# Scaling keys and queries on VectorE alone in a hybrid decoder layer

## The chip, the cores and the metric

The kernel runs on one core of a Trainium2 chip. The core has a matrix engine (TensorE, PE in the profile), three engines for elementwise work (VectorE or DVE, ScalarE or ACT, GpSimd or POOL), a queue processor that issues transfers (SyncE or SP), and 16 DMA engines. The metric is device time in microseconds, lower is better.

## The reference

One decoder layer over 512 tokens of width 1024, in float32. A normalised input is projected to many columns at once; four token mixers of width 512 work on them (A: forgetting attention with 8 heads of 64, B: a gated linear recurrence, C: sparse attention with 8 query heads over 2 key heads, D: spatial gating), each is gated, projected back, merged by sigmoid gates, and a last projection is added to the input. What the change touches is the RMS normalisation of the attentions' queries and keys, each head's 64 values by themselves:

```python
def rms_norm(x, g):
    x32 = x.astype(jnp.float32)
    y = x32 * lax.rsqrt(jnp.mean(x32 * x32, axis=-1, keepdims=True) + NORM_EPS)
    return (y * g.astype(jnp.float32)).astype(x.dtype)
...
    y_a = fox_attention(rms_norm(heads(qa, FOX_HEADS), qn_a), rms_norm(heads(ka, FOX_HEADS), kn_a),
                        heads(va, FOX_HEADS), fa + b_forget).reshape(B, S, W)
    y_c = nsa_attention(rms_norm(heads(qc, NSA_HEADS), qn_c), ...
```

In attention C the keys of the selected and of the windowed branch are normalised the same way.

## The kernel before, in words

**Precision.** Every operand of a product is split into a high part, rounded for TensorE, and a low part, the difference; a product is high x high, high x low and low x high. For a weight the high part (`hi_cast`) is a copy by GpSimd or ScalarE and the low part a VectorE subtraction in two halves of 512 columns (`wsplit`, tiles `w_...` from `r_...`). Both inputs of that subtraction lie in SBUF.

**Stages.** The projections to `ka`, `qa` and `va` come first, from about 6 to 78 us, 128 tokens to a PSUM bank. `emit_z` copies each bank to `zk_a` or `zq_a`, squares it and sums the squares of each head. `fox_scales` turns the sums into reciprocal square roots (tile `tsa`, a run of short VectorE instructions) and multiplies each token block of `zk_a` (lines 729 to 732: 128 partitions, 8 heads of 64) and of `zq_a` by its scales, in place. In the same region `gate_block` computes the forget gate's logarithms (`fa`) and their running sum, the scan that writes `negc`, a part of the tile `y_a`; its value goes into rows of the keys' operand `kb_a`.

Attention A then runs head by head (`fox_units`, `attend`) from about 77 to 180 us. Its TensorE instructions are interleaved with those of dense projections that don't depend on it: `kv`, `qc`, `cm`, `vd`. For a head: keys and queries are transposed on TensorE (`kt_a`, `qt_a`), scores go to `s_a`, VectorE adds the mask and takes the minimum of the negated scores (`p_a`, `nm_a`), ScalarE takes the exponential, GpSimd scales the rows, TensorE transposes them (`tb`), ScalarE and VectorE split them (`ph_a`, `pl_a`), TensorE multiplies with the values into the one bank of `o_a`. `evict` empties that bank: ScalarE copies one half (`ol_a`), VectorE adds the other (`y_a`); only then may the next head write to the bank.

Attention C's keys (`zk_c`, a part of the tile `zkm`, 4 heads) and queries (`zq_c`, 8 heads) come out of the `kv` and `qc` projections in that time. Once the last `qc` block is there, the generator `nsa_scales` is put on the list `side`, whose generators advance between matmuls; it computes the scales (tile `tsc`) and multiplies, token block by token block, `zk_c` (256 columns) and `zq_c` (512 columns). TensorE transposes them (`kt_s`, `kt_w`, `qt_c`) once attention A is done.

**What sets the order.** From line 609 to line 1390 an instruction isn't issued where it is written: `Order.add` notes it with what it depends on, and `Order.settle` issues a region after `Order.plan` has ordered each engine's queue. The plan takes four drafts of a list schedule; each draft takes on every engine the instruction that is due first, by a due time worked back from TensorE's order in the draft before. Costs are in `Order.cost`. An instruction of GpSimd other than a memset, or of VectorE with an SBUF input and none in PSUM, is taken to hold a shared port, so that the draft lets one engine begin after the other's instruction. The lines of it that bear on the scalings:

```python
        if name == "DVE":
            alone = bool(wide) and method not in ("tensor_reduce", "reciprocal", "memset") and not any(
                x.tensor.name in self.psum for x in wide)
            return 0.155 + free / 960 + 0.05 * scalar + 0.06 * (method == "tensor_tensor_scan" and free / 100), alone
...
        return (0.09 + free / 540 if len(wide) > 1 and method == "tensor_tensor" else 0.18 + free / 1170), True
```

On TensorE a draft takes, of the instructions that are ready, the one that the program text has first. On the chip the engines run their queues in order and wait for each other by semaphores. From about 365 us on the order is that of the program text.

**Transfers.** SP issues the weights' loads, each behind the VectorE subtraction that frees its buffer. GpSimd issues the transfers that add in memory (`dmg0s`, `dmg2s` and the like), paced by TensorE's progress.

In the profile nearly all instructions of the ordered region carry line 290, that of the issuing call, so tiles tell them apart. The functions that the change touches:

Of the kernel before, what the change touches and what calls it, by code (L numbers as in the profile page):

```python
# [14 lines left out]
ALU = mybir.AluOpType  # L15
# [3 lines left out]
P = 128  # L19
# [306 lines left out]
def tile_hybrid_layer(ctx: ExitStack, tc: tile.TileContext, x, xT, units, small, bsp, out):  # L326
    nc = tc.nc
    order = Order(nc)
    ACT, DVE, POOL, PE, DMA = (_Engine(order, e) for e in ("ACT", "DVE", "POOL", "PE", "SP"))
# [259 lines left out]
    def rsqrt(v, y, t):  # L589

        I32 = mybir.dt.int32
        DVE.tensor_scalar(t.bitcast(I32), v.bitcast(I32), 1, None, op0=ALU.logical_shift_right)
        DVE.tensor_scalar(y.bitcast(I32), t.bitcast(I32), -1.0, float(0x5F3759DF), op0=ALU.mult, op1=ALU.add)
        for _ in range(3):
            DVE.tensor_tensor(t, y, y, op=ALU.mult)
            DVE.scalar_tensor_tensor(t, t, -0.5, v, op0=ALU.mult, op1=ALU.mult)
            DVE.scalar_tensor_tensor(y, t, 1.5, y, op0=ALU.add, op1=ALU.mult)
# [104 lines left out]
    zk_a = rp.tile([P, 4, S], F32, name="zk_a")  # L702
    zq_a = rp.tile([P, 4, S], F32, name="zq_a")
# [19 lines left out]
    def fox_scales():  # L723
        DVE.tensor_tensor(ssa, ssa, rstd[:, 1, :].unsqueeze(2).to_broadcast([P, 4, 16]), op=ALU.mult)
        DVE.tensor_scalar(ssa, ssa, EPS, None, op0=ALU.add)
        y = tsa[:, 0, :].rearrange("p (t h) -> p t h", t=4)
        rsqrt(ssa, y, tsa[:, 1, :].rearrange("p (t h) -> p t h", t=4))
        DVE.tensor_tensor(y, y, rstd[:, 0, :].unsqueeze(2).to_broadcast([P, 4, 16]), op=ALU.mult)
        for t in range(4):
            for z, c0, eng in ((zk_a, 0, POOL), (zq_a, 8, DVE)):  # L730
                zv = z[:, t, :].rearrange("p (h d) -> p h d", h=8)
                eng.tensor_tensor(zv, zv, y[:, t, c0:c0 + 8].unsqueeze(2).to_broadcast([P, 8, 64]), op=ALU.mult)

# [92 lines left out]

    run(gv, 8)
    fox_scales()
    gate_block()
    run(gv)  # L830
# [159 lines left out]
    def nsa_scales():  # L990
        DVE.tensor_scalar(ssc, ssc, 1.0 / 64, EPS, op0=ALU.mult, op1=ALU.add)
        y_ = tsc[:, 0, :].rearrange("p (t h) -> p t h", t=4)
        rsqrt(ssc, y_, tsc[:, 1, :].rearrange("p (t h) -> p t h", t=4))
        yield 0.0
        for t in range(4):
            for z, c0, n in ((zk_c, 0, 4), (zq_c, 4, 8)):
                zv = z[:, t, :].rearrange("p (h d) -> p h d", h=n)
                POOL.tensor_tensor(zv, zv, y_[:, t, c0:c0 + n].unsqueeze(2).to_broadcast([P, n, 64]), op=ALU.mult)
                yield 0.0
                yield 0.0  # L1000

# [25 lines left out]
    def last_qc(t, ps):  # L1027
        emit_qc(t, ps)
        if t == 3:
            side.append(nsa_scales())  # L1030
# [957 lines left out]
```

## Time and profile before

| | |
|---|---|
| median of 3 runs (lowest to highest) | 695.24 us (694.14 to 695.49) |
| the profiled execution: its time, its span | 695.5 us, 693.8 us |
| mean granted TensorE clock | 0.997 |
| busy: TensorE, VectorE, ScalarE, GpSimd | 683.2, 553.4, 406.5, 209.4 us |
| GpSimd's scalings of `zk_a` | 4, 5.8 us |
| GpSimd's scalings of `zq_c` and `zkm` | 4 and 4, 4.9 and 3.0 us |
| VectorE's scalings of `zq_a` | 4, 5.0 us |

Busy times overlap, since the engines work side by side. A busy TensorE is not one at its peak, because matmuls are pipelined and their ends are modelled. The difference between the execution's time and its span, 1.7 us, lies around the profiled instructions. In the rows below, a group has its engine, operation, the tiles written and read (out<-in), shapes and count, then busy time and mean duration, then the idle time in front of it and what ended that. A row of a timeline has start and length in us; idle time before it stands in brackets with what ended it.

### The profile page before, as it was taken

How to read it: one execution, taken by the hardware profiler on the slowest of the kernel's cores; microseconds unless marked ns; L12 is line 12 of the kernel's file. 1: busy time of each engine (PE TensorE's matmuls, PEld its weight loads, DVE VectorE, ACT ScalarE, POOL GpSimd, SP SyncE). 2: the span in 40 equal slices, each digit the busy share in tenths (PEclk: the TensorE clock that was granted, in tenths of full speed). 3: DMA queues.
4: the chain of work that ended last, by engine and by line, in shares of the span. 5: the costliest groups of instructions: out<-in, count | busy, mean ns of one | idle time of the engine just before them, and what ended most of it. 6: DMA issues, size and time to landing. Idle time of an engine off the chain costs nothing.

```text
span 693.8 us, 9785 instructions
## 1 busy us (share of the span) xinstructions
PE 683.2 (98%) x3277; PEld 564.5 (81%) x3277; DVE 553.4 (80%) x1100; ACT 406.5 (59%) x766; POOL 209.4 (30%) x279
## 2 busy tenths in 40 slices
PE   8999999998999999999999999999999999999997
PEld 6888788886888787888887878888888888888886
DVE  6789788696668648889998579977889788858995
ACT  4563558574272237777666894355666665655861
POOL 4114864546445324534351121200202401300000
PEclk9999999999999999999999999999999999999999
DMA  8637176798869999964202225459999999896422
GB/s 310 256 122 242 40 203 212 225 218 234 249 183 318 253 312 221 247 167 106 62 31 77 78 89 188 162 187 358 252 331 311 366 317 363 234 339 207 132 90 92
DMA packets 35298, 145.44 MB, mean 210 GB/s; under 512 B 4128, under 2 KB 7584, under 8 KB 32032
## 3 DMA queue, kind: packets, MB, share of 16 engines
q1 hardware_dynamic: 30208, 108.67, 43.8%
q0 software_dynamic: 4608, 35.65, 24.0%
q10 hardware_dynamic: 432, 0.49, 0.3%
q8 instruction: 26, 0.43, 0.2%
q14 instruction: 24, 0.20, 0.1%
HBM read 139.56 MB, written 58.20 MB: 285 GB/s over the span
## 4 chain that ended last, share of the span: by engine, by line
PE 91%; ACT 3%; DVE 3%; POOL 1%; DMA 1%; issue 1%; SPq 0%; DVEq 0%; POOLq 0%; ACTq 0%
PE pj L302 4%; PE tb L290 3%; PE z_ka L290 3%; PE z_qc L290 3%; PE z_xb L290 3%; PE z_ga L290 3%; PE z_va L290 3%; PE z_vd L290 3%; PE z_gd L290 3%; PE z_gb L302 3%; PE z_qa L290 3%; PE z_ud L290 3%; PE z_kv L290 3%; PE o_s L290 3%; PE outy L302 3%; PE mg0y L302 2%
## 5 line engine op out<-in xcount | busy, mean ns | idle before, releaser
L302 POOL TENSOR_SCALAR mark<-mark 128x1 f32<-128x1 f32 x16 | 16.8, 1050 | 102.8 <-ACT mark L302 102.7
L302 DVE TENSOR_TENSOR w_mg<-r_mg,w_mg 128x512 fp32r<-128x512 f32 x48 | 31.8, 687 | 11.1 <-ACT w_mg L302 11.0
L302 PE MATMUL pj<-w_wb,yh 128*128 128x512 f32 x128 | 40.4, 390 | 0.0
L302 ACT CAST w_mg<-r_mg 128x1024 fp32r<-128x1024 f32 x24 | 25.2, 1049 | 10.3 <-issue 4.9
L290 POOL TENSOR_SCALAR p_s<-p_s,nm_s 128x512 f32<-128x512 f32 (+3 forms) x32 | 21.3, 681 | 22.4 <-DVE nm_s L290 18.5
L302 PEld LDWEIGHTS pj<-w_wb,yh 128*128 128x128 f32 x128 | 24.0, 188 | 4.9
L290 POOL TENSOR_SCALAR p_w<-p_w,nm_w 128x128 f32<-128x128 f32 (+3 forms) x32 | 18.4, 588 | 29.9 <-DVE nm_w L290 29.9
L290 ACT ACTIVATE p_s<-p_s,nm_s 128x512 f32<-128x512 f32 (+3 forms) x32 | 18.0, 562 | 13.6 <-DVE nm_s L290 13.2
L302 PE MATMUL pj<-w_wb,yl 128*128 128x512 f32 x64 | 25.4, 396 | 0.5 <-DVE yl L302 0.5
L290 ACT ACTIVATE p_w<-p_w,nm_w 128x256 f32<-128x256 f32 (+3 forms) x32 | 17.9, 562 | 12.4 <-DVE nm_w L290 12.3
L290 PE MATMUL z_xb<-xh,w_xb 128*128 128x512 f32 x64 | 24.6, 410 | 0.0
L290 POOL TENSOR_SCALAR p_a<-p_a,nm_a 128x128 f32<-128x128 f32 (+3 forms) x32 | 19.0, 607 | 16.5 <-DVE nm_a L290 16.4
L290 ACT CAST ph_a<-tb 128x512 fp32r<-128x512 f32 (+1 forms) x24 | 12.4, 516 | 19.3 <-PE tb L290 19.1
L290 PE MATMUL z_ud<-xh,w_ud 128*128 128x512 f32 x64 | 23.4, 405 | 0.0
L290 PE MATMUL z_gd<-xh,w_gd 128*128 128x512 f32 x64 | 22.6, 397 | 0.3 <-DVE sgd L290 0.3
L290 PE MATMUL z_ga<-xh,w_ga 128*128 128x512 f32 x64 | 21.9, 397 | 0.0
L302 DVE TENSOR_TENSOR w_wb<-r_wb,w_wb 128x512 fp32r<-128x512 f32 x28 | 18.5, 687 | 4.0 <-POOL w_wb L302 3.5
L302 PE MATMUL z_gb<-xh,w_gb 128*128 128x512 f32 x64 | 20.9, 390 | 0.0
L290 ACT ACTIVATE p_a<-p_a,nm_a 128x512 f32<-128x512 f32 (+3 forms) x32 | 17.9, 560 | 5.1 <-DVE nm_a L290 5.1
L302 POOL TENSOR_SCALAR w_wb<-r_wb 128x1024 fp32r<-128x1024 f32 x8 | 10.0, 1250 | 28.9 <-PE pj L302 13.9
L290 DVE CUSTOM_DVE_ANT_0 p_a<-s_a,maskm 128x512 f32<-128x512 f32 (+3 forms) x32 | 14.9, 486 | 4.6 <-PE tb L290 2.8
L290 ACT CAST ph_s<-tb 128x512 fp32r<-128x512 f32 (+1 forms) x24 | 12.2, 512 | 9.0 <-PE tb L290 8.7
(744 smaller groups left out, 2413.1 us busy)
## 6 DMA issues: line engine op xcount, KB each, us to landing
r_mg<-in_units_dram SPq DMA_DIRECT2D x16, 512.0 KB, 6.9
r_wb<-in_units_dram SPq DMA_DIRECT2D x12, 512.0 KB, 3.7
dmg<-in_units_dram POOLq DMA_DIRECT2D x4, 1024.0 KB, 9.7
r_mg<-dmg SPq DMA_DIRECT2D x8, 512.0 KB, 10.1
dmg0s<-in_units_dram POOLq DMA_DIRECT2D x3, 1024.0 KB, 10.5
dmg2s<-in_units_dram POOLq DMA_DIRECT2D x3, 1024.0 KB, 13.6
dmg1s<-in_units_dram POOLq DMA_DIRECT2D x3, 1024.0 KB, 11.4
r_mg0s<-dmg0s SPq DMA_DIRECT2D x6, 512.0 KB, 4.6
```

The lines of the kernel that those rows point to most:

```text
L290: getattr(self.eng[name], method)(*args, **kw)
L302: return lambda *args, **kw: real(*args, **kw).ins
```

## The change

The engine of twelve multiplications changes: in `fox_scales` those of `zk_a` (4 of 128 x 512), in `nsa_scales` those of `zk_c` and `zq_c` (4 of 128 x 256 and 4 of 128 x 512). Operands, shapes and the order in the program text stay; the order in the queues is planned anew from the changed program.

```diff
@@ fox_scales
         for t in range(4):
-            for z, c0, eng in ((zk_a, 0, POOL), (zq_a, 8, DVE)):
+            for z, c0, eng in ((zk_a, 0, DVE), (zq_a, 8, DVE)):
                 zv = z[:, t, :].rearrange("p (h d) -> p h d", h=8)
                 eng.tensor_tensor(zv, zv, y[:, t, c0:c0 + 8].unsqueeze(2).to_broadcast([P, 8, 64]), op=ALU.mult)
@@ nsa_scales
             for z, c0, n in ((zk_c, 0, 4), (zq_c, 4, 8)):
                 zv = z[:, t, :].rearrange("p (h d) -> p h d", h=n)
-                POOL.tensor_tensor(zv, zv, y_[:, t, c0:c0 + n].unsqueeze(2).to_broadcast([P, n, 64]), op=ALU.mult)
+                DVE.tensor_tensor(zv, zv, y_[:, t, c0:c0 + n].unsqueeze(2).to_broadcast([P, n, 64]), op=ALU.mult)
```

## The prediction

> **What bounds the kernel now.** I read the page first, for the engine that sets the end.
>
> ```profile
> span 693.8 us, 9785 instructions
> PE 683.2 (98%) x3277; PEld 564.5 (81%) x3277; DVE 553.4 (80%) x1100; ACT 406.5 (59%) x766; POOL 209.4 (30%) x279
> PE 91%; ACT 3%; DVE 3%; POOL 1%; DMA 1%; issue 1%; SPq 0%; DVEq 0%; POOLq 0%; ACTq 0%
> ```
>
> TensorE is busy for 98% of the span and is 91% of the chain that ends last. So time can only come from moments in which TensorE stands still or runs slowly, and the second view is its list of waits, of which these are the longest:
>
> ```profile
> PE o_a L290 <- DVE y_a L290: 2.7, 1, 2.7
> PE warm L302 <- DVE warm L302: 1.5, 1, 1.5
> PE tb L290 <- POOL p_w L290: 0.5, 1, 0.5
> ```
>
> The longest is one single wait of 2.7 us, for VectorE. Everything else is small or belongs to the start. The third view, busy time by stretches, shows what lies around it (columns: stretch, length, busy time and count of PE, PEld, DVE, ACT, POOL, then granted clock, DMA share, GB/s).
>
> ```profile
> 157.00:163.00 6.00, 3.34 (x19) 2.57 (x17) 5.94 (x9) 3.65 (x12) 3.49 (x5) 1.00 0.91 314
> 163.00:165.00 2.00, 1.93 (x9) 1.69 (x10) 1.63 (x3) 0.94 (x2) 1.09 (x1) 0.79 1.02 176
> 165.00:167.50 2.50, 2.50 (x7) 1.92 (x7) 0.69 (x1) 0.19 (x1) 2.50 (x6) 0.50 0.72 131
> 167.50:170.00 2.50, 2.50 (x16) 2.20 (x15) 0.13 (x1) 1.70 (x3) 2.50 (x4) 0.98 0.16 33
> 170.00:196.50 26.50, 26.50 (x125) 22.03 (x125) 14.94 (x38) 8.82 (x16) 8.51 (x16) 1.00 0.85 238
> 196.50:300.00 103.50, 102.52 (x533) 84.06 (x531) 79.67 (x200) 53.85 (x133) 46.11 (x59) 1.00 0.93 256
> 300.00:365.00 65.00, 64.89 (x374) 55.28 (x374) 61.49 (x173) 44.80 (x116) 27.21 (x43) 1.00 0.32 78
> ```
>
> After the gap the granted clock is 0.79, 0.50 and 0.98 before it is 1.00 again: the gap has a tail. Then TensorE runs without a gap to 196.5, and nearly so to 365. The fourth view, the timeline of single engines, tells what made VectorE late. TensorE:
>
> ```profile
> 159.96 0.39 PE L290 MATMUL z_cm<-xl,w_cm 128*128 128x512 f32 x1
> 163.07 0.47 PE L290 MATMUL o_a<-ph_a,v_a 128*128 128x512 f32 x1 [2.73 <-DVE y_a L290]
> ```
>
> VectorE, ScalarE and GpSimd:
>
> ```profile
> 157.07 3.97 DVE L290 TENSOR_TENSOR w_vd.01_961<-r_vd.01_960,w_vd.01_961 128x512 fp32r<-128x512 f32 x1
> 160.97 0.41 DVE L290 CUSTOM_DVE_ANT_0 p_a<-s_a,maskm 128x256 f32<-128x256 f32 x1
> 161.53 0.68 DVE L290 TENSOR_TENSOR w_vd.01_961<-r_vd.01_960,w_vd.01_961 128x512 fp32r<-128x512 f32 x1
> 162.24 0.68 DVE L290 TENSOR_TENSOR y_a<-o_a,ol_a 64x512 f32<-64x512 f32 x1
> ...
> 158.09 0.59 ACT L290 COPY ol_a<-o_a 64x512 f32<-64x512 f32 x1 [0.17 <-PE o_a L290]
> ...
> 157.03 0.91 POOL L290 TENSOR_TENSOR zkm<-zkm,tsc 128x256 f32<-128x256 f32 x1
> 157.61 1.32 POOL L290 TENSOR_TENSOR zq_c<-zq_c,tsc 128x512 f32<-128x512 f32 x1
> 158.61 0.89 POOL L290 TENSOR_TENSOR zkm<-zkm,tsc 128x256 f32<-128x256 f32 x1
> 159.18 1.31 POOL L290 TENSOR_TENSOR zq_c<-zq_c,tsc 128x512 f32<-128x512 f32 x1
> ```
>
> Here is the whole mechanism. The same subtraction takes 0.68 us at 161.53 and 3.97 us at 157.07. During the long one GpSimd runs four of the scalings that the change moves, from 157.03 to 160.49, and VectorE's instruction ends at 161.04, 0.55 us behind the last of them. In the queue behind it stand two score reductions, the second subtraction and y_a, which empties the one PSUM bank that the next head's values need. ScalarE had handed over its part at 158.68 (158.09 + 0.59); y_a starts only at 162.24.
>
> **The change part by part: the second attention (line 998).** The change takes eight scalings from GpSimd and gives them to VectorE.
>
> What goes. Without GpSimd's scalings the subtraction at 157.07 takes 0.68 and ends at 157.75. The two reductions take 0.56 (160.97 to 161.53), the second subtraction 0.68: VectorE reaches y_a at about 159.0 (later than ScalarE's 158.68, so VectorE decides) and ends it at 159.7. TensorE is busy until 160.35 (159.96 + 0.39), so it doesn't wait, with 0.65 us to spare. That is the 2.73 us. The clock's tail: a stretch of t us at clock c loses t(1 - c), so 2.0 x 0.21 + 2.5 x 0.50 + 2.5 x 0.02 = 0.42 + 1.25 + 0.05 = 1.72 us. The tail is contiguous with the gap and every later stretch shown has 1.00, so I let it go with the gap. Gain: 2.73 + 1.72 = 4.45 us.
>
> What comes. Eight multiplications on VectorE, bounded by these rows:
>
> ```profile
> L290 DVE TENSOR_TENSOR w_ga<-r_ga,w_ga 128x512 fp32r<-128x512 f32 x8 | 5.4, 698 | 3.2 <-POOL w_ga L290 2.5 <-ACT w_ga L290 0.7
> L290 DVE TENSOR_TENSOR sc<-sc,cm 128x256 f32<-128x256 f32 x8 | 3.5, 432 | 0.2
> L290 PE MATMUL kt_s<-identf,zkm x4: 272/272/273, 196.6 to 197.0; 128*128 128x128 f32 x4
> L290 PE MATMUL qt_c<-identf,zq_c x16: 270/272/273, 198.5 to 324.7; 128*128 128x128 f32 x16
> ```
>
> Four of 512 columns at 0.70 and four of 256 at 0.43 are 4.5 us. Their first readers are transposes on TensorE at 196.6 and 198.5, 39 us after GpSimd begins with them at 157.03. In the 33.5 us from 163.0 to 196.5 VectorE is busy 1.63 + 0.69 + 0.13 + 14.94 = 17.4 us, so 16 us are free: cover of three times the need, and I take 0 for them. Without cover they would cost up to 4.5 us, or, if each meets a GpSimd instruction as zq_a does below (1.53 for 512 columns; 0.91, GpSimd's slowest, for 256), 4 x 1.53 + 4 x 0.91 = 9.8 us. Below zero the cost can't go: they free nothing that this sum doesn't count already. No DMA is issued by the moved step; GpSimd's queue merely gets past it sooner.
>
> A page of the Trainium skill, "SBUF — State Buffer", section "Who interferes with whom", says that a VectorE instruction with two SBUF inputs and a GpSimd instruction that reads SBUF lock each other out, and that whoever is first holds the ports for one whole instruction. The row agrees with the lockout, not with its length: VectorE lost 3.3 us (3.97 - 0.68), and no single GpSimd instruction there lasted over 1.32. By the page alone 1.32 us of the delay would go and 2.0 stay, of which 1.3 us would still reach TensorE: a gain of some 1.4 us instead of 2.73, and 694.1. The end times (160.49 and 161.04) speak for all four scalings as the cause.
>
> **The first attention (lines 730 to 732).** Four of GpSimd's scalings join VectorE's four.
>
> ```profile
> L290 POOL TENSOR_TENSOR zk_a<-zk_a,tsa x4: 1478/1485/1487, 64.0 to 68.4; 128x512 f32<-128x512 f32 x4
> L290 DVE TENSOR_TENSOR zq_a<-zq_a,tsa x4: 691/1526/1532, 63.9 to 67.4; 128x512 f32<-128x512 f32 x4
> 63.92 5.04 DVE L290 TENSOR_TENSOR zq_a<-zq_a,tsa 128x512 f32<-128x512 f32 x4
> 71.30 1.21 DVE L290 TENSOR_TENSOR_SCAN y_a<-fm,fa 8x512 f32<-8x512 f32 x1 [0.69 <-ACT fa L290]
> 78.82 0.60 ACT L290 CAST kb_a<-y_a 8x512 fp32r<-8x512 f32 x1
> L290 PE MATMUL kt_a<-identf,zk_a x16: 271/272/273, 77.9 to 137.2; 128*128 128x128 f32 x16
> ```
>
> Both engines slow each other to about 1.5 us a piece now, so VectorE needs 5.04 us for four. Eight alone at the uncontended 0.691 of the same row are 5.5 us: VectorE is 0.5 us later at most, and GpSimd is free 5.8 us (68.4 + 1.49 - 64.0) earlier. Behind VectorE stand the forget gate's logarithm and its scan at 71.30; the scan ends at 72.51 and its reader starts at 78.82, so 6 us cover half a microsecond. TensorE reads zk_a at 77.9, 8 us after it is done now. Cost 0; if all four met GpSimd work at 1.53, another 3.4 us, still covered; a gain is excluded, since TensorE waits for nothing there.
>
> **Sum.** 695.5 us is the profiled execution's own time (span 693.8 and 1.7 around it), 0.3 above the median of 695.24. 695.5 - 4.45 = 691.05; I say 691.0. All later work follows TensorE, so it moves forward with it.
>
> **The rivals.**
>
> *The gap goes, the clock's tail stays.* If the tail had another cause, 695.5 - 2.73 = 692.8. For it: the gap is only 2.73 us long. Against: the tail begins where the gap ends, and the stretches shown from 170 on have none. "TensorE: Matmul & The Clock Gate" of the Trainium skill, section "What's actually happening", lets the clock fall after an idle window of about 3.4 us, which by its letter this gap doesn't fill; it calls that window free-running. Chance 0.06.
>
> *Only part of the gain arrives, or it is given back.* The transfers could take it: their share is 0.85 to 0.93 from 170 to 300, and weights that land no earlier would make TensorE wait for what it no longer waits for at 160; then 695.5. Against: no TensorE wait above names a DMA. The plan of the whole region is also drawn anew, with VectorE busy 61.49 of 65 us from 300 to 365; one new gap of about 2.7 us with its tail would give the gain back too. Chance 0.15, centre 695; the 694.1 of the shorter lockout lies in it.
>
> *Slower: the scalings are queued ahead of y_a.* The scales are ready by 157.03, where VectorE has 0.65 us to spare. All eight there at 4.5 us give y_a's end at 164.2 and a gap of 3.9 against 2.73 now, with the tail 1.2 us slower: 696.7. Contended at 9.8 us the gap is 9.2 us: 6.4 us slower, 702. It decides from 0.65 + 2.73 = 3.4 us of scalings in front of y_a. For it: the plan already puts the w_vd.01 subtractions there, though other work could go first. Against: the plan ranks by due time, and 196.6 is late. Chance 0.11.
>
> *More is gained.* GpSimd, freed at 64, and VectorE, freed at 166, shorten small stalls up to 365: 689.5. Chance 0.08. That the change doesn't do what it says I leave out: the engine is written in the call.
>
> **How the numbers follow.** The forecast (690 to 692.5) has 0.60. Within 0.2% of 695.24, that is 693.85 to 696.65, is about what a measurement of this kernel can't tell from no change. Faster: 0.60 + 0.06 + 0.08 = 0.74. Same: 0.15. Slower: 0.11. The range from 689.0 to 696.0 leaves out the slower case, the upper end of the part-gain case and the far end of the last one, 0.2 together.
>
> **What would show it.** Right, if the profile after has no GpSimd TENSOR_TENSOR on zk_a, zkm and zq_c, both w_vd.01 subtractions near 0.7 us, no TensorE wait for y_a over 0.5 us, a clock of 1.00 through the stretch around 165, and the first kt_s transpose some 4.4 us earlier, near 192. The first attention's transpose of zk_a should stay at 77.9. Wrong, if scalings stand between the tsc work and y_a on VectorE, if w_vd.01 still takes over 1.5 us, or if kt_s comes earlier but the end doesn't: then a later stage has given it back.

## The result and the profile after

| | before | after |
|---|---|---|
| median (lowest to highest) | 695.37 us (694.14 to 695.54) | 690.51 us (690.42 to 691.71) |
| the profiled execution: time, span | 695.5, 693.8 us | 690.54, 688.8 us |
| mean granted clock of it | 0.997 | 0.999 |

The ratio of the times is 0.9938, with a 95% interval from 0.9921 to 0.9955: 4.3 us faster on that scale, 4.9 by the medians. The forecast was 691.0 within 689.0 to 696.0.

The page of the changed kernel first, the rows that were shown of before:

```profile
span 688.8 us, 9783 instructions
PE 680.0 (99%) x3277; PEld 563.2 (82%) x3277; DVE 550.9 (80%) x1112; ACT 406.7 (59%) x766; POOL 198.8 (29%) x267
PE 92%; ACT 3%; DVE 2%; POOL 1%; DMA 1%; issue 1%; SPq 0%; DVEq 0%; POOLq 0%; ACTq 0%
```

Twelve instructions have moved from POOL (279 to 267) to DVE (1100 to 1112). VectorE has more instructions and yet less busy time, 550.9 against 553.4 us: a first sign that its old time was in part time locked out. TensorE lost 3.2 us of busy time with the same 3277 matmuls: 1.7 us is what the low clock cost before, 1.0 us lies in the first 78 us (75.1 us busy there, 76.1 before), where its work is the same, and the rest was not traced further. Its waits, longest first (waiter, releaser, us in total, times, longest):

```profile
PE warm L302 <- DVE warm L302: 1.5, 1, 1.5
PE z_ka L290 <- POOL w_ka.00_154 L290: 1.4, 1, 1.4
```

The wait of `o_a` for `y_a`, 2.7 us before, isn't there. The wait for the first weight (`z_ka`) belongs to the start of the run and differs from execution to execution, 0.3 to 1.4 us in the profiles of this case. The same stretches as before (length, busy time and count of PE, PEld, DVE, ACT, POOL, clock, DMA share, GB/s):

```profile
157.00:163.00 6.00, 6.00 (x34) 5.12 (x33) 5.94 (x15) 4.61 (x13) 2.34 (x3) 1.00 0.83 282
163.00:165.00 2.00, 2.00 (x14) 1.69 (x13) 2.00 (x5) 1.32 (x2) 2.00 (x3) 1.00 1.05 180
165.00:167.50 2.50, 2.50 (x17) 2.17 (x15) 2.35 (x5) 0.59 (x3) 1.12 (x2) 1.00 1.06 197
167.50:170.00 2.50, 2.50 (x13) 2.08 (x12) 1.60 (x4) 2.40 (x4) 0.00 (x0) 1.00 1.01 200
300.00:365.00 65.00, 64.89 (x371) 54.88 (x370) 59.98 (x167) 42.84 (x112) 27.59 (x44) 1.00 0.28 70
```

TensorE is busy 6.00 of 6.00 us where it was busy 3.34, with 34 matmuls where there were 19, and the clock is 1.00 throughout. The last row shows that the region's end has the same 0.11 us of idle TensorE as before: nothing is given back there. The timeline of VectorE, TensorE and GpSimd around the old gap:

```profile
157.00 0.68 DVE L290 TENSOR_TENSOR w_vd.01_961<-r_vd.01_960,w_vd.01_961 128x512 fp32r<-128x512 f32 x1
158.16 0.69 DVE L290 TENSOR_TENSOR w_vd.01_961<-r_vd.01_960,w_vd.01_961 128x512 fp32r<-128x512 f32 x1
158.88 0.69 DVE L290 TENSOR_TENSOR y_a<-o_a,ol_a 64x512 f32<-64x512 f32 x1
...
164.41 0.68 DVE L290 TENSOR_TENSOR zq_c<-zq_c,tsc 128x512 f32<-128x512 f32 x1
...
160.11 0.39 PE L290 MATMUL o_a<-ph_a,v_a 128*128 128x512 f32 x1
...
160.88 4.48 POOL L290 TENSOR_SCALAR p_a<-p_a,nm_a 128x384 f32<-128x384 f32 x4 [3.66 <-DVE nm_a L290]
```

Both subtractions take 0.68 to 0.69 us, `y_a` ends at 159.57, and the next `o_a` product starts at 160.11 with no wait in brackets. The eight scalings were planned right behind `y_a`: the first starts at 160.2 (`zkm` in the tiles below), the last, shown here, ends at 165.09. That is not the freer time after 166. The last row is a thing that the prediction didn't have: GpSimd's row scalings `p_a`, four in a group, take 4.48 us beside VectorE's multiplications. GpSimd's timeline before has the same group at 2.60 us, and behind it two scalings that had VectorE mostly idle beside them:

```profile
163.91 2.60 POOL L290 TENSOR_SCALAR p_a<-p_a,nm_a 128x384 f32<-128x384 f32 x4 [3.42 <-DVE nm_a L290]
166.48 0.60 POOL L290 TENSOR_TENSOR zkm<-zkm,tsc 128x256 f32<-128x256 f32 x1
167.06 1.03 POOL L290 TENSOR_TENSOR zq_c<-zq_c,tsc 128x512 f32<-128x512 f32 x1
```

The slowing now works the other way round, and TensorE doesn't wait for it.

Last the tiles (shortest, median and longest in ns, first start to last start):

```profile
L290 DVE TENSOR_TENSOR zk_a<-zk_a,tsa x4: 685/686/693, 63.8 to 67.4; 128x512 f32<-128x512 f32 x4
L290 DVE TENSOR_TENSOR zq_a<-zq_a,tsa x4: 686/688/690, 64.4 to 68.0; 128x512 f32<-128x512 f32 x4
L290 DVE TENSOR_TENSOR zkm<-zkm,tsc x4: 408/416/507, 160.2 to 164.0; 128x256 f32<-128x256 f32 x4
L290 DVE TENSOR_TENSOR zq_c<-zq_c,tsc x4: 661/678/992, 160.6 to 164.4; 128x512 f32<-128x512 f32 x4
L290 PE MATMUL kt_a<-identf,zk_a x16: 270/272/273, 77.8 to 137.1; 128*128 128x128 f32 x16
L290 PE MATMUL kt_s<-identf,zkm x4: 272/272/273, 192.0 to 192.4; 128*128 128x128 f32 x4
L290 PE MATMUL qt_c<-identf,zq_c x16: 270/272/273, 193.9 to 319.9; 128*128 128x128 f32 x16
```

`kt_a` starts at 77.8 (77.9 before), `kt_s` at 192.0 (196.6 before), the last `qt_c` at 319.9 (324.7). So 0.1 of the 5.0 us by which the span is shorter is there before attention A begins, 4.5 more by 192, and some 0.4 us comes behind it.

### The profile page after: what moved, and what is told of

It reads as the page before. It is cut to its first block, busy times and chain, and to the rows that moved or that the text cites. A ratio compares the mean times of both kernels' runs of the same rounds, so it can differ in the third digit from the quotient of the medians.

```text
span 688.8 us, 9783 instructions
## 1 busy us (share of the span) xinstructions
PE 680.0 (99%) x3277; PEld 563.2 (82%) x3277; DVE 550.9 (80%) x1112; ACT 406.7 (59%) x766; POOL 198.8 (29%) x267
## 4 chain that ended last, share of the span: by engine, by line
PE 92%; ACT 3%; DVE 2%; POOL 1%; DMA 1%; issue 1%; SPq 0%; DVEq 0%; POOLq 0%; ACTq 0%
PE pj L302 4%; PE tb L290 4%; PE z_qc L290 3%; PE z_ka L290 3%; PE z_xb L290 3%; PE z_ga L290 3%; PE z_va L290 3%; PE z_vd L290 3%; PE z_gd L290 3%; PE z_gb L302 3%; PE z_qa L290 3%; PE z_ud L290 3%; PE z_kv L290 3%; PE o_s L290 3%; PE outy L302 3%; PE mg0y L302 2%
## 5 line engine op out<-in xcount | busy, mean ns | idle before, releaser
L290 POOL TENSOR_SCALAR p_a<-p_a,nm_a 128x128 f32<-128x128 f32 (+3 forms) x32 | 20.9, 666 | 16.8 <-DVE nm_a L290 16.7
L302 DVE SCALAR_TENSOR_TENSOR pj<-tg,pj 128x512 f32<-128x512 f32 x24 | 16.5, 688 | 1.3 <-ACT tg L302 1.3
```

The costliest lines, as they stand in the source:

```text
L290: getattr(self.eng[name], method)(*args, **kw)
L302: return lambda *args, **kw: real(*args, **kw).ins
```

## The experiments

The theory on record: four GpSimd scalings in a row hold VectorE's subtraction, that delays `y_a`, the gap in TensorE lowers its clock for a while, and the scalings cost VectorE nothing. Its rivals: the clock falls for another reason, the newly planned order is what helps, the moved work costs something, or the lockout is shorter than four instructions. The kernels ran in three groups on two chips, each together with the kernel before; a ratio compares within a group. The kernel before had medians of 695.51 and 695.4 us on the first chip and of 694.74 us on the other, where the kernels below with the scalings on GpSimd and the one with five fillers ran.

**Each half alone.** For the second attention alone:

```diff
@@ line 998, nsa_scales
-                POOL.tensor_tensor(zv, zv, y_[:, t, c0:c0 + n]...
+                DVE.tensor_tensor(zv, zv, y_[:, t, c0:c0 + n]...
```

> Only the eight scalings of attention C go to VectorE; those of zk_a stay on GpSimd. Theory (a port collision at 157 us makes y_a late, the gap of 2.7 us and its slow-clock tail of 1.7 us are the whole gain): all of the change's gain, 690.5, within 0.5. Rival (the first attention's freed GpSimd gives the half microsecond that the sum lacked): 691.0 or more, and kt_a later than in the changed kernel by some tenths.

Measured: 690.75 us (690.7 to 691.43), ratio 0.9937 (0.9923 to 0.9952). For the first attention alone:

```diff
@@ line 730, fox_scales
-            for z, c0, eng in ((zk_a, 0, POOL), (zq_a, 8, DVE)):
+            for z, c0, eng in ((zk_a, 0, DVE), (zq_a, 8, DVE)):
```

> Only the four scalings of zk_a go to VectorE. Theory: no change, 695.4, within 0.5, the gap at 160 to 163 and its tail still there, although eight scalings now take VectorE about 4.9 us where four took 5.04. Rival: 694.9 or less.

Measured: 695.56 us (693.98 to 696.39), ratio 1.000 (0.9988 to 1.0012). Its wait list, its subtractions and three stretches:

```profile
PE o_a L290 <- DVE y_a L290: 2.7, 1, 2.7
...
L290 DVE TENSOR_TENSOR w_vd.01_961<-r_vd.01_960,w_vd.01_961 x2: 681/2328/3974, 157.2 to 161.7; 128x512 fp32r<-128x512 f32 x2
...
163.00:165.00 2.00, 1.80 (x6) 1.45 (x7) 1.72 (x4) 0.66 (x2) 0.97 (x1) 0.59 0.97 176
165.00:167.50 2.50, 2.50 (x10) 2.08 (x9) 0.69 (x1) 0.59 (x1) 2.50 (x6) 0.65 0.84 164
167.50:170.00 2.50, 2.50 (x16) 2.15 (x15) 0.00 (x0) 1.54 (x3) 2.50 (x4) 1.00 0.10 20
```

The whole effect lies in line 998, and the four scalings of `zk_a` change the time by nothing that shows. The stretches say something more. The gap is the same 2.7 us and ends at 163.20 here (163.07 before), but the clock falls at another moment: 2.0 x 0.41 + 2.5 x 0.35 = 1.7 us are lost, as before, half of it now ahead of 165. So in these two executions the low clock has the same length and doesn't begin at a fixed distance from the gap.

**The order of before, the scalings on VectorE.** The plan is made as before, and only when it is issued does a scaling go to VectorE, at the place that it had in the plan:

```diff
@@ line 290, Order.settle
-            getattr(self.eng[name], method)(*args, **kw)
+            getattr(self.eng[self.moved.get(i, name)], method)(*args, **kw)
@@ line 998
-                POOL.tensor_tensor(zv, zv, ...)
+                order.moved[POOL.tensor_tensor(zv, zv, ...)] = "DVE"
```

> The order of before on every engine, planned as for GpSimd; only when it is issued does each of the eight scalings of attention C go into VectorE's queue, at its place in the old order. One of 256 and one of 512 columns then stand ahead of y_a. Theory: no lockout, y_a 0.9 us later than the 159.6 of the changed kernel, so a stall of 0.2 to 0.4 us and 690.9, no tail. Rival (the newly drawn order gives the gain, not the engine): 695.4. Rival (scalings ahead of y_a cost what was forecast for the slower case): over 696.

Measured: 691.84 us (691.03 to 692.41), ratio 0.995 (0.9934 to 0.9967).

```profile
PE o_a L290 <- DVE y_a L290: 0.4, 1, 0.4
...
L290 DVE TENSOR_TENSOR w_vd.01_961<-r_vd.01_960,w_vd.01_961 x2: 680/684/687, 157.5 to 159.0; 128x512 fp32r<-128x512 f32 x2
...
158.13 0.42 DVE L290 TENSOR_TENSOR zkm<-zkm,tsc 128x256 f32<-128x256 f32 x1
159.62 0.68 DVE L290 TENSOR_TENSOR zq_c<-zq_c,tsc 128x512 f32<-128x512 f32 x1
160.34 0.68 DVE L290 TENSOR_TENSOR y_a<-o_a,ol_a 64x512 f32<-64x512 f32 x1
```

Without GpSimd beside them the subtractions are short in the old order too, so the order isn't what removes the gap. Two scalings, 0.42 + 0.68 = 1.10 us, stand ahead of `y_a` and cost TensorE 0.4: the rival "queued ahead of y_a" is real, in small. That leaves about 0.7 us of spare time in front of `y_a`, against 0.65 by the prediction.

**The order of before, no scalings.** The eight of the second attention are planned and not issued:

```diff
@@ line 290
-            getattr(self.eng[name], method)(*args, **kw)
+            if i not in self.some[0:]: getattr(self.eng[name], method)(*args, **kw)
@@ line 998
-                POOL.tensor_tensor(zv, zv, ...)
+                order.some.append(POOL.tensor_tensor(zv, zv, ...))
```

> The order of before, with the eight scalings of attention C left out when they are issued (its keys and queries stay unscaled). It prices the collision alone, without eight scalings on VectorE and without a new order. Theory: 690.6, within 0.5: the gap and the tail go, and the eight scalings on VectorE cost nothing. Rival (the new order gives 0.5 us of the gain): 691.0 to 691.3. Rival (scalings on VectorE cost something in the changed kernel): 690.0 or less.

Measured: 691.02 us (690.62 to 692.44), ratio 0.9943 (0.9928 to 0.9958). With the scalings on VectorE the time is 690.75 in the newly planned order (second attention alone) and 691.84 in this old order. So in one and the same order VectorE's scalings cost some 0.8 us by the medians, 0.4 of it the wait for `y_a`, with ranges that overlap; in the new order they cost nothing that shows against a kernel without them, but the new order without scalings was not run.

**The scalings on GpSimd, later.** The plan of before, but the eight are held back until GpSimd has cast the first half of `w_ga`, at about 179, away from the subtractions. Line 290 keeps them aside and issues them there, line 998 marks them, line 446 (`hi_cast`) marks the cast:

```diff
@@ line 290
-            getattr(self.eng[name], method)(*args, **kw)
+            self.stash.append((method, args, kw)) if i in self.held else getattr(self.eng[name], method)(*args, **kw); [getattr(self.eng["POOL"], m)(*a, **k) for m, a, k in (self.stash if i == self.mark else ())]
```

> GpSimd keeps all scalings, and every other instruction keeps the order of before; the eight of attention C merely stand later in GpSimd's queue, behind its high-part copy of the weight ga at about 178 to 183 us, after the last y_a. Theory (the collision, not the engine, costs the time): 690.9, within 0.5, no gap, no tail; the lockout moves to the ga subtractions at 179, which are not needed for some ten us. Rival (GpSimd is too slow for these scalings): 694 or more, with kt_s waiting for GpSimd. Rival (any lockout of this size costs a gap): 695.

Measured: 694.9 us, ratio 1.0006 (0.9988 to 1.0024): the forecast was missed by 4 us. The old gap is gone, and others have come:

```profile
PE z_ga L290 <- DVE w_ga L290: 1.6, 1, 1.6
...
PE s_s L290 <- DVE q_c L290: 0.8, 1, 0.8
...
L290 DVE TENSOR_TENSOR w_vd.01_961<-r_vd.01_960,w_vd.01_961 x2: 683/685/687, 157.1 to 158.3; 128x512 fp32r<-128x512 f32 x2
...
179.28 2.55 DVE L290 TENSOR_TENSOR w_ga<-r_ga,w_ga 128x512 fp32r<-128x512 f32 x2 [2.46 <-POOL w_ga L290]
...
179.22 0.61 POOL L290 TENSOR_TENSOR zkm<-zkm,tsc 128x256 f32<-128x256 f32 x1
179.80 1.48 POOL L290 TENSOR_TENSOR zq_c<-zq_c,tsc 128x512 f32<-128x512 f32 x1
...
187.61 1.05 POOL L290 TENSOR_SCALAR tblk<-trs 128x1024 fp32r<-128x1024 f32 x1
...
188.70 1.23 DVE L290 TENSOR_TENSOR tblk<-trs,tblk 128x1024 fp32r<-128x1024 f32 x1 [5.35 <-POOL tblk L290]
...
196.65 1.71 DVE L290 TENSOR_TENSOR w_ga<-r_ga,w_ga 128x512 fp32r<-128x512 f32 x2
```

The eight fill GpSimd's queue from 179.22 to 186.5 and push what stands behind them: GpSimd's part of `tblk` starts at 187.61, at 180.23 in the changed kernel. VectorE's part waits 5.35 us for it, all that stands behind it in VectorE's queue is late too, and the next pair of `w_ga` subtractions starts at 196.65 instead of 192.42; for these TensorE waits the 1.6 us at 197.4. `kt_s` doesn't wait, so the rival with that sign is not what happened. Moving the collision to this place is not enough: GpSimd's 7.3 us for this work cost time there.

The first pair of `w_ga` subtractions shows something else. They took 2.55 us for two, 1.29 in the changed kernel, although eight scalings follow each other beside them: the pair ended at 181.83, long before the row of scalings did (186.5). Here the two engines took turns, and VectorE lost 1.3 us on two subtractions where at 157 it lost 3.3 us on one. The instructions have the same shapes in both places.

**The order of after, the scalings on GpSimd.** The edit of line 290 as above, with the changed kernel's plan and `"POOL"` in place of `"DVE"`.

> The order of the changed kernel on every engine, but the eight scalings of attention C are run by GpSimd, at their places in that order: one of 256 and one of 512 columns stand right behind its transfer at 156.4, free to start at 157, the others are mixed with the row scalings p_a. Theory: two scalings collide with the w_vd.01 subtraction instead of four, which holds it for about 1.6 us more; y_a ends at about 161.2, a gap of 0.9 us, no tail or a short one, and some small stalls because p_a is later: 692.2, between 691.5 and 694. Rival (the newly drawn order gives the gain): 690.6.

Measured: 693.19 us (691.94 to 693.9), ratio 0.9973 (0.996 to 0.9985).

```profile
PE o_a L290 <- DVE y_a L290: 1.5, 2, 1.1
...
L290 DVE TENSOR_TENSOR w_vd.01_961<-r_vd.01_960,w_vd.01_961 x2: 681/1546/2412, 157.1 to 159.9; 128x512 fp32r<-128x512 f32 x2
...
157.02 0.90 POOL L290 TENSOR_TENSOR zkm<-zkm,tsc 128x256 f32<-128x256 f32 x1
157.59 1.32 POOL L290 TENSOR_TENSOR zq_c<-zq_c,tsc 128x512 f32<-128x512 f32 x1
162.33 0.58 POOL L290 TENSOR_SCALAR p_a<-p_a,nm_a 128x384 f32<-128x384 f32 x1 [3.42 <-DVE nm_a L290]
```

In this order GpSimd has two scalings in a row ahead of `p_a` instead of four, and the subtraction takes 2.41 instead of 3.97 us. With the scalings on GpSimd the order is thus worth part of the gain, and the engine the rest: a ratio of 0.9973 here, 0.9938 for the changed kernel.

**Two scalings.** The plan of before; GpSimd runs the first two and the other six are left out (`some[2:]` in the edit of line 290 above).

> The order of before; of the eight scalings of attention C only the first two, 256 and 512 columns, are run, by GpSimd, and six are left out. Theory (GpSimd keeps the port over instructions that follow each other at once): the w_vd.01 subtraction lasts until both are done, at about 158.9, so 2.0 to 2.4 us instead of 3.97; y_a ends at about 161.2, a gap of 0.9 us; span 690 to 691. Rival (one instruction at a time holds the port, and the other engine comes next): the subtraction starts behind the first, 0.6 us long, and lasts 1.2 to 1.5 us, no gap; span 689.1.

Measured: 692.23 us in one execution.

```profile
157.24 0.90 POOL L290 TENSOR_TENSOR zkm<-zkm,tsc 128x256 f32<-128x256 f32 x1
157.81 1.32 POOL L290 TENSOR_TENSOR zq_c<-zq_c,tsc 128x512 f32<-128x512 f32 x1
...
157.28 2.42 DVE L290 TENSOR_TENSOR w_vd.01_961<-r_vd.01_960,w_vd.01_961 128x512 fp32r<-128x512 f32 x1
```

VectorE's instruction ends at 159.70, 0.57 us behind the last scaling (159.13); with four in the kernel before it was 0.55 behind (161.04 and 160.49). Length 3.97 with four, 2.42 with two, 0.68 with none: at this place VectorE comes to its end only when GpSimd's row of multiplications has ended, not after one of them. The row is slowed as well: 0.90 and 1.32 us for what takes 0.60 and 1.03 with VectorE idle.

**A gap without a collision.** The changed kernel, with fillers on VectorE (sums over `maskm` into an unused tile, 0.71 us each) in front of the same `y_a`; the range is 3, 4, 5 or 6:

```diff
@@ line 290
-            getattr(self.eng[name], method)(*args, **kw)
+            self.first.get(i, lambda: None)(); getattr(self.eng[name], method)(*args, **kw)
@@ line 970, evict
+ ...; order.first.update({last["dve"]: lambda: [nc.vector.tensor_reduce(fit[:, 0:8], maskm.rearrange("p (h d) -> p h d", h=8), axis=AX.X, op=ALU.add) for _ in range(5)]} if name == "a5" else {})
```

> The changed kernel with five extra VectorE instructions of 0.6 us each, sums of the mask that nothing reads, right ahead of the y_a of the sixth head: y_a is 3.0 us later, at about 162.6, and TensorE stands still for about 2.3 us. It measures the clock's tail by itself, with no port collision. Theory (the gap causes the tail): the granted clock falls to 0.5 for about 3.4 us, 1.7 us lost, and the span is 4.0 us over the 688.8 of the changed kernel, 692.8. Rival (the tail had another cause than the gap): clock 1.00, span 691.1. Open: whether a gap this much under 2.7 us still does it.

Measured: 699.08 us in one execution (span 697.4), far above the forecast. The wait is 2.9 us, and the clock stays low for twice as long:

```profile
PE o_a L290 <- DVE y_a L290: 2.9, 1, 2.9
...
163.00:165.00 2.00, 1.19 (x3) 1.02 (x4) 1.97 (x5) 0.00 (x0) 0.02 (x1) 0.51 1.20 229
165.00:167.50 2.50, 2.50 (x10) 2.01 (x9) 2.19 (x4) 0.59 (x1) 2.50 (x3) 0.50 0.90 180
167.50:170.00 2.50, 2.50 (x8) 2.02 (x7) 2.20 (x5) 0.00 (x0) 1.49 (x3) 0.53 0.64 88
```

2.0 x 0.49 + 2.5 x 0.50 + 2.5 x 0.47 = 3.4 us, twice the 1.7 of before; since TensorE was busy for only 1.19 of the first 2.0 us, about 3.0 of them were lost. GpSimd runs nothing there that collides, so a gap alone lowers the clock. Gap and clock make 5.9 of the 8.6 us by which this span is over the changed kernel's; 0.6 more is there when attention A begins (`kt_a` at 78.4), and 2.0 come behind 198, cause open. Is it the gap's length that decides? Three more:

> The changed kernel with three fillers of VectorE, 0.71 us each, in front of the same y_a (2.1 us, of which some 0.6 are spare): a TensorE wait for y_a of about 1.5 us. Theory that the tail's length follows the gap's length alone: a gap of 1.6 us left none elsewhere, so every execution has a mean clock of 0.999 or 1.000 and the time is 692.1 us. Theory that the clock is decided by the share of idle time in windows of 3.41 us that run by themselves, so that it depends on where the gap falls in them: a few executions in ten show 0.998 or less, the rest not; median still 692.1, up to 693 with stalls that follow.

> Four fillers, 2.8 us: a TensorE wait for y_a of about 2.2 us, between the 1.6 that left no tail and the 2.7 of the kernel before. By length alone all executions are alike: all without a tail (clock 0.999 to 1.000, 692.8 us, up to 693.7 with stalls that follow) or all with one window at half speed (0.997, 694.5 us). By windows that run by themselves the executions differ: some at 0.997, some at 0.999 to 1.000, and their times stand about 1.7 us apart.

> Six fillers, 4.3 us: a TensorE wait for y_a of about 3.6 us, longer than one window of 3.41 us. By length alone all executions have two windows at half speed, as the gap of 2.9 us had (clock 0.994 to 0.995, 690.5 + 3.6 + 3.4 = 697.5 us, and 1 to 2 us of stalls that follow: 699). By windows that run by themselves nearly every execution has one or two, mixed: 0.997 and 0.995, about 1.7 us apart, and none at 0.999 or more.

Measured: waits for `y_a` of 1.5, 2.2 and 3.6 us, as forecast; medians 693.16, 694.8 and 697.2 us, ratios 0.9971 (0.9961 to 0.9981), 0.9991 (0.9981 to 1.0002) and 1.0033 (1.002 to 1.0046). The executions of one kernel are not alike. A window of 3.4 us at half clock lowers the mean clock of the run by 1.7 / 694 = 0.0025, so executions with one show 0.998 or less:

| gap | kernel | executions at 0.998 or less |
|---|---|---|
| none to 0.4 us | changed kernel, second attention alone, the two on the old order | 0 of 16 |
| 1.1 us, then 0.4 us | GpSimd in the order of after | 0 of 10 |
| 1.2 us | two scalings | 0 of 1 |
| 1.5 us | three fillers | 0 of 11 |
| 1.6 us, then 0.8 us | GpSimd later | 2 of 10 |
| 2.2 us | four fillers | 8 of 11 |
| 2.7 us | kernel before | 33 of 53 (12 of 13 and 13 of 21 on one chip, 8 of 19 on the other) |
| 2.7 us | first attention alone | 8 of 10 |
| 2.9 us | five fillers | 1 of 1, at 0.994 |
| 3.6 us | six fillers | 5 of 5, two of them at 0.995 |

The gaps are those of each kernel's profiled execution.

Executions of one kernel differ at 2.2, 2.7 and 3.6 us, so the theory of the gap's length alone falls. Windows that run by themselves would explain the spread, if whether a gap costs clock depends on where in a window it falls; but no run here shows where in a window the gap fell in the executions without a low clock, and that theory's forecast for three fillers, a low clock in a few executions of ten, was missed (0 of 11). The shares also differ between groups of one and the same kernel, the one before, so they are no constants of a gap's length. With four fillers the profiled execution is one of the three above 0.998: its wait and the stretch behind it, at a clock of 1.00.

```profile
PE o_a L290 <- DVE y_a L290: 2.2, 1, 2.2
...
163.00:165.00 2.00, 2.00 (x11) 1.70 (x12) 2.00 (x6) 0.59 (x1) 0.85 (x1) 1.00 0.93 156
```

The two executions of "GpSimd later" with a low clock took 698.4 and 698.6 us, some 4 us more than the others; what else held those is open.

## Why the prediction was right, point by point

*The long subtraction comes from four GpSimd scalings.* Shown: 3.97, 2.42 and 0.68 us with four, two and none. "SBUF — State Buffer" of the Trainium skill, section "SBUF: two separate sides", lets whichever starts first have the ports for one whole instruction; by that rule VectorE would have lost no more than 1.32 us beside two scalings, and it lost 1.74 (2.42 - 0.68). The measurement decides: at 157 us the delay grows with the number of consecutive GpSimd multiplications. At 179 us, with the scalings held back, it didn't: there a pair of subtractions lost 1.3 us in all, no more than that rule allows for one scaling in front of each. What makes the one place differ from the other is open.

*It is what TensorE waited for, 2.73 us, with 0.65 us to spare.* Shown. The wait is gone in each kernel whose subtractions are short and where nothing was put in front of `y_a`, and has 1.1 to 1.2 us in those whose subtraction takes 2.4. The spare time comes out again from the fillers: 3.56 - 2.91 = 0.65 us.

*The clock's tail goes with the gap.* Shown as to its cause (the gap of the fillers brings it without a collision), mis-sized as to its certainty. The prediction took 1.72 us from one profiled execution as belonging to the kernel; 20 of the 53 executions of before had no tail. The median of these 20 is 694.28, that of the other 33 is 695.73; with four fillers the medians are 694.1 without and 695.08 with a low clock. Nor did the tail begin, in the profile before, where the gap ends, as the prediction has it: 0.42 us lost ahead of 165 are 0.84 us at half clock, so it began at about 164.2, 1.1 us behind the gap. On average the tail is worth 1.45 x 33 / 53 = 0.9 us; the median of before fell among the executions with it. "TensorE: Matmul & The Clock Gate" of the Trainium skill, section "What's actually happening", has the clock fall after an idle window of about 3.4 us and calls the window free-running; the low clock's length agrees (1.7 us lost at half clock), and the spread over executions fits it. That the window must be idle as a whole doesn't agree: a gap of 2.2 us lowered the clock in 8 of 11 executions.

*The scalings cost VectorE nothing.* Borne out, though not isolated: 690.75 with eight on VectorE in the new order is no more than 691.02 without any in the old one, and what they might cost or the new order save by itself was not separated. They were not put where the prediction saw 16 us free, but right behind `y_a`, so the reason given for the 0 is not the one at work: behind `y_a` no TensorE wait shows for them, and the delay that they bring to GpSimd's `p_a` (4.48 for 2.60 us) reaches none either.

*The first attention changes nothing.* Shown: 695.56 against 695.51. In detail the direction was wrong: VectorE was said to be done up to 0.5 us later. In the changed kernel the eight follow each other every 0.60 us and take 4.9 us, and the next instruction, `fa`, has no GpSimd work beside it (0.41 us for 1.72), so that the scan starts at 69.75 instead of 71.30. (The time by which GpSimd is free earlier, 68.4 + 1.49 - 64.0, is 5.9 us and not 5.8; nothing rests on it.)

*The sum.* 4.45 us were forecast, 4.96 came in the profiled executions (695.5 to 690.54). Against the executions of before without a tail the gain is 694.28 - 690.51 = 3.8 us, of which the gap is 2.73: about 1 us more than the gap itself. So the sum came near for two errors that nearly cancel, which is in part luck: the tail was counted at 1.72 and is worth 0.9 on average, and about 1 us was not counted at all. The fillers show that extra too: a gap of 1.5 us costs 693.16 - 690.51 = 2.65 us, without any tail. In the profile of three fillers, its slowest execution (694.24 us), more than that lies between the first `qt_c` and the last, 127.6 us against 126.0 in the changed kernel:

```profile
L290 PE MATMUL qt_c<-identf,zq_c x16: 270/272/273, 195.9 to 323.5; 128*128 128x128 f32 x16
```

With four fillers the same stretch takes 126.0 us (196.8 to 322.8), and with five 128.0. So the extra is not at one place, and which waits make it is open. The rival "more is gained" had the direction of it; its mechanism, an earlier GpSimd and an earlier VectorE, isn't shown, and the first attention alone, with GpSimd free earlier, gained nothing.

*Slower, if the scalings are queued ahead of y_a.* The mechanism exists: two ahead of it cost 0.4 us of wait. The plan put all eight behind, as the prediction expected from the due times.

## What to carry to other kernels

One long VectorE instruction among short ones of its kind, with a row of GpSimd two-tensor work beside it, is the sign of a lockout. Its price can be the length of the whole row (as at 157 us) or about one instruction (as at 179 us), so read it from the end times, and it matters if its engine's queue leads to the bottleneck. Moving the same GpSimd work to one other time only moved the wait here, while giving it to VectorE (4.8 us, the eight lengths added, for GpSimd's 7.3) removed it. Where TensorE is the bound, count a stall of over 2 us with a low clock behind it (1.7 us here), with a chance and not as a certainty, and read the mean clock of several executions, not of one.

## What the runs showed of the hardware that was not expected

- The slowing is mutual, and who loses more differs: four row scalings of GpSimd took 4.48 us beside VectorE's multiplications, 2.60 before; VectorE's subtraction took 3.97 us beside four scalings; in the first attention before, both engines took about 1.5 us a piece, in turns; and with the scalings held back to 179 us, two subtractions got through a row of eight scalings in 2.55 us. What decides between these wasn't settled.
- The granted clock falls in portions: 1.7 us lost or twice that, at places not tied to the gap (half of it ahead of 165 in one profile, most of it behind 165 in another, after equal gaps). Between gaps of 1.5 and 2.2 us the share of executions with a low clock rose from 0 of 11 to 8 of 11.
- By the medians a gap of TensorE came with about 1 us more than its length, even with the clock at 1.00 (2.65 us for 1.5, in a kernel whose VectorE also had 2.1 us of fillers). Its place is open.
